# A causal depthwise convolution as a 287-point transform on TensorE, with scale and shift formed k-tile by k-tile beside the first product

## The chip, the cores and the metric

The kernel runs on one core of a Trainium2 chip. The metric is device microseconds of one execution; a lower number is better. In this text PE is TensorE (matmuls) and PEld its weight loads, DVE is VectorE, ACT is ScalarE, POOL is GpSimd, and SP is SyncE, whose queue issues every large transfer. Each engine works through its own instructions in the order in which they were written out.

## The reference

Two layers work on 256 tokens of 2048 channels in float32. Layer 0 mixes tokens with a convolution module, layer 1 with gated linear attention; behind each mixer stands a feed-forward block. The part that matters here is the beginning of layer 0:

```python
mod = silu(c) @ w_ada[i] + b_ada[i]                 # c: one row of 2048; w_ada: 2048 x 12288
sh1, sc1, gt1, sh2, sc2, gt2 = split(mod, 6)
h = rms_norm(x, pre_mix_g[i]) * (1.0 + sc1) + sh1
u = h @ w_pw1 + b_pw1                               # 2048 -> 4096, "pw1"
a, g = split(u, 2); u = a * sigmoid(g)
u = depthwise_conv(u, w_dw, 31 taps, causal) + b_dw # each channel by itself
u = silu(layer_norm(u, ln_g, ln_b))
y = u @ w_pw2 + b_pw2                               # 2048 -> 2048, "pw2"
x = x + gt1 * rms_norm(y, post_mix_g[i])
h = rms_norm(x, pre_ffn_g[i]) * (1.0 + sc2) + sh2   # then the feed-forward block
```

The products are computed with float32 split in two parts of reduced precision, hi and lo, as hi·hi + hi·lo + lo·hi. A causal convolution of 256 tokens with 31 taps has 286 outputs, so a circular transform of 287 points holds it without wrapping.

## The kernel before, in words

Channels lie on the 128 partitions in 16 k-tiles, tokens along the row. All weights come from HBM as tiles of 128 x 2048 numbers (1 MiB), in one long list that `tile_order()` writes out by hand; `pump_one()` takes the next entry, issues its transfer on SP and writes the work that goes with it. There are six buffers (`rawp`), so a transfer waits until the sixth tile before it has been used. A weight tile of a product is turned into two halves of hi (a cast on ACT, L281) and lo (a subtraction, L282); for pw1 the subtraction is on POOL, for all other products on DVE. `product()` runs the matmuls of one product in the order of `ORDERS`; for pw1 the weights are the stationary operand and 256 tokens stream through (L342, L343, L348), so its output has channels as rows.

Scale and shift (`mod`) come in two ways. An `ada` tile holds the weights of 128 outputs and is one DVE instruction (L260), a product with silu(c) and a sum along the row. An `adap` tile is k-tile k of a whole chunk of 2048 outputs and goes through PE (`ada_rows`, L214): silu(c) is the stationary operand in 32 columns, and four matmuls of 512 columns go to four column groups of the array. Of layer 0, SC1 and SH1 are `ada` tiles at the very start; GT1, SC2 and SH2 are `adap` tiles beside pw1 and pw2. As soon as all of SC1 and a block of SH1 are there, `modulate()` forms h of one k-tile: mt on DVE (L414), hi on ACT (L417), lo on DVE (L418).

The convolution follows pw1 block by block (`conv_done`): a sigmoid and a bias on ACT, their product on POOL or DVE, and then 31 taps, each one DVE instruction on 128 x 256 numbers into PSUM (L623, L604 for the last two blocks, where 4 and 12 taps are diagonal matmuls on PE, L591). Mean and mean square of the layer norm are gathered on PE (`conv_sums`, L567). Behind the last block a short chain forms the normalisation, and pw2 begins (L318 to L320 in packed blocks, L345 and L348 after them). `gather()` collects what the junction needs: sums of y, z and x·z. The junction `j0` forms the next h, and the first feed-forward product starts (the tile `in_pair`).

The scheduler of the tile framework sets the final order on each engine; blocks marked with `tc.high_priority` are drawn forward.

Of the kernel before, what the change touches and what calls it, by code (L numbers as in the profile page):

```python
# [34 lines left out]
PE_TAPS = {KD - 2: 4, KD - 1: 12}  # L35
# [3 lines left out]
PE_CHUNKS = (GT1, SC2, SH2)  # L39
PW1_GROUP = 4  # L40
# [7 lines left out]
PW1_OBS = [ob for i in range(KD) for ob in (i, KD + i)]  # L48
# [3 lines left out]
def ffn_in_obs(half):  # L52
# [4 lines left out]
    "pw1": block_order(PW1_OBS, KD, PW1_GROUP),  # L57
# [24 lines left out]
def tile_order():  # L82
# [40 lines left out]
def trunk(ctx: ExitStack, tc: tile.TileContext, a: dict, out: bass.AP):  # L123
# [15 lines left out]
    early = pre.enter_context(tc.tile_pool(name="early", bufs=1))  # L139
    ccol = early.tile([P, KD], F32, tag="ccol", name="ccol")  # L140
    nc.sync.dma_start(out=ccol, in_=a["ccol"])
    cc = early.tile([P, KD, 32], F32, tag="cc", name="cc")
    ident = const.tile([P, P], F32, tag="ident", name="ident")
    x = const.tile([P, KD, T], F32, tag="x", name="x")
    par = const.tile([P, NCOLS], F32, tag="par", name="par")
    masks = const.tile([P, 8, P], I8, tag="masks", name="masks")
# [8 lines left out]
    quad = early.tile([P, 4], F32, tag="quad", name="quad")  # L155
    nc.vector.memset(quad, 0.0)
    for j in range(4):
        nc.vector.memset(quad[32 * j : 32 * j + 32, j : j + 1], 1.0 / 32)
# [16 lines left out]
    der = const.tile([P, 8, KD], F32, tag="der", name="der")  # L175

# [21 lines left out]
    def chunk_done(layer, chunk):  # L198
        m = modcol(layer, chunk * KD, KD)
        kinds = {SC1: (0, "pre_mix_g"), GT1: (1, "post_mix_g"), SC2: (2, "pre_ffn_g"), GT2: (3, "post_ffn_g")}  # L200
        if chunk in kinds:
            kind, g = kinds[chunk]
            nc.vector.scalar_tensor_tensor(
                out=der[:, layer * 4 + kind, :], in0=m, scalar=1.0 if kind in (0, 2) else 0.0,
                in1=cols(g, layer * KD, KD), op0=ALU.add, op1=ALU.mult,
            )

    rows = {}

    def ada_rows(raw, n, k):  # L210
        if k == 0:
            rows[n] = ps2.tile([P, 512], F32, tag="ss", name=f"ada{n}")
        for j in range(4):
            nc.tensor.matmul(  # L214
                rows[n][32 * j : 32 * j + 32, :], cc[:, k, :], raw[:, j * 512 : (j + 1) * 512],
                start=k == 0, stop=k == KD - 1,
            )
        if k < KD - 1:
            return
        got = rows.pop(n)  # L220
        flat = rawp.tile([P, TILE * P], F32, tag="raw", name=f"flat{n}")[:, :512]
        nc.scalar.copy(flat, got)
        pc = ps2.tile([P, 512], F32, tag="ss", name=f"adac{n}")[:, :KD].rearrange("p (j s) -> p s j", j=4)
        for s in range(4):
            nc.tensor.matmul(pc[:, s, :], flat[:, s * P : (s + 1) * P], quad, start=True, stop=True)
        chunk = PE_CHUNKS[n]
        nc.vector.tensor_tensor(
            out=modcol(0, chunk * KD, KD).rearrange("p (j s) -> p j s", j=4), in0=pc.rearrange("p s j -> p j s"), in1=cols("b_ada", chunk * KD, KD).rearrange("p (j s) -> p j s", j=4),
            op=ALU.add
        )  # L230
        chunk_done(0, chunk)
# [5 lines left out]
    def pump_one():  # L237
        kind, name, i = order[state["next"]]
        state["next"] += 1
        if kind == "x":  # L240
            nc.sync.dma_start(out=x, in_=a["x"])
            return
        if kind == "par":
            nc.sync.dma_start(out=par, in_=a["par"])
            nc.sync.dma_start(out=ident, in_=a["ident"])
# [7 lines left out]
        if kind == "adap":  # L253
            nc.sync.dma_start(out=raw, in_=a["w_ada_d"][name, i])
            waiting.append((state["emitted"], lambda: ada_rows(raw, name, i)))
            return
        if kind == "ada":
# [5 lines left out]
            if i % KD == KD - 1 or (name, i // KD) == (0, SH1):  # L263
                first = i if i // KD == SH1 and name == 0 else i - KD + 1
# [4 lines left out]
                if i % KD == KD - 1:  # L269
                    chunk_done(name, i // KD)  # L270
            if (name, i // KD) == (0, SH1):
                modulate(i % KD, rbx, 0, 0, SH1)
            return
        nc.sync.dma_start(out=raw, in_=a[name][i])
        on_pool = name == "pw1"
        eng = nc.gpsimd if on_pool else nc.vector
        for j in range(2):
# [4 lines left out]
            done = eng.tensor_tensor(out=lo, in0=part, in1=hi.bitcast(F32), op=ALU.subtract)  # L282
            last_lo[:] = [] if on_pool else [done.ins]
# [160 lines left out]
    def gather_on(stack, ob, name, yo, **kw):  # L444
# [8 lines left out]
        else:  # L453
            square_into(s_y, yo, f"{name}_y{ob}", ob == 0, **bias)
        nc.vector.tensor_scalar(
            out=z, in0=yo, scalar1=kw.get("bias", 0.0), scalar2=aa, op0=ALU.add, op1=ALU.mult
        )
# [58 lines left out]
    ssx = None  # L516
    pump(-1)
    while order[state["next"]][0] != "w" and order[state["next"]] != ("ada", 0, SH1 * KD):
        pump_one()
    ssx = new_ss("ssx")[:, :2]  # L520
    for k in range(KD):
        sq = new_sq(f"x_sq{k}")
        nc.scalar.square(sq, x[:, k, :])
        sum_sq(ssx, sq, inv_d, k == 0, k == KD - 1)
    rbx = rstd(ssx, "nx")

    with tc.tile_pool(name="conv", bufs=1) as cv:
        dw = cv.tile([P, KD, WIDTH], F32, tag="dw", name="dw")
        nc.sync.dma_start(out=dw, in_=a["dw"])
        uc = cv.tile([P, KD, T], F32, tag="uc", name="uc")  # L530
        up = [cv.tile([P, PAD + T], F32, tag=f"up{i}", name=f"up{i}") for i in range(4)]
        for u in up:
            nc.vector.memset(u[:, :PAD], 0.0)
        w128 = cv.tile([P, P], F32, tag="w128", name="w128")
        nc.vector.memset(w128, 1.0 / P)
        base = cv.tile([P, T], F32, tag="base", name="base")
        stat = {}
        first = {}
        later = []
# [417 lines left out]
```

## Time and profile before

| | |
|---|---|
| median of three runs | 2446.92 us (2445.59 to 2451.66) |
| the profiled execution | 2445.52 us, of which its span 2443.7 us |
| PE busy | 2340.2 us, 96% of the span |
| DVE busy | 1832.0 us, 75% |
| ACT, POOL busy | 1112.5 us, 200.4 us |
| read from HBM | 599.89 MB, 246 GB/s over the span |

Busy shares are means over the span. The span begins with the first instruction. An engine that is busy may still be waited for by none; what a stage costs is read from the chain of waits, which goes back from the last instruction and says at each step what released it. A matmul's length in the profile is a modelled one that overlaps with the next; the distance from one start to the next is what it costs in a row of them.

### The profile page before, as it was taken

The numbers are of one execution on the slowest core, as the hardware profiler recorded it, in microseconds if no ns is written. First come the engines' busy times: TensorE is split into PE (matmuls) and PEld (weight loads), VectorE is DVE, ScalarE is ACT, GpSimd is POOL, SyncE is SP. The second block draws the span as 40 slices with busy tenths as digits, with TensorE's granted clock in tenths as the row PEclk, the third lists the DMA queues.
The fourth block names the chain that finished last, engine by engine and source line by source line (L and its number), as shares of the span: only waits on it lengthen the run. The fifth ranks groups of instructions, "written<-read, shape, count | busy, mean of one in ns | idle before, by whom it ended". The sixth has DMA issues, their size and how long they took to land.

```text
span 2443.7 us, 36498 instructions
## 1 busy us (share of the span) xinstructions
PE 2340.2 (96%) x14554; PEld 2051.4 (84%) x14554; DVE 1832.0 (75%) x2784; ACT 1112.5 (46%) x1679; POOL 200.4 (8%) x118
## 2 busy tenths in 40 slices
PE   3599999899999999999999999999999999999997
PEld 2588868798888888888888989988988888888886
DVE  7988876887777677878986987889666655665665
ACT  2244425554444444444445545454444444444442
POOL 0377730000000000000000000000000000000001
PEclk9899999899999999999999999999999999999999
DMA  9877788557778777877843566784556665665651
GB/s 396 333 277 261 273 334 294 199 176 289 286 286 303 288 290 294 294 293 290 297 172 138 207 256 233 285 295 140 207 207 225 223 218 211 224 218 202 220 189 68
DMA packets 84157, 604.36 MB, mean 247 GB/s; under 512 B 9473, under 2 KB 9857, under 8 KB 11025
## 3 DMA queue, kind: packets, MB, share of 16 engines
q1 hardware_dynamic: 83986, 602.02, 67.5%
q8 instruction: 114, 1.87, 0.3%
q14 instruction: 57, 0.47, 0.1%
HBM read 599.89 MB, written 2.10 MB: 246 GB/s over the span
## 4 chain that ended last, share of the span: by engine, by line
PE 93%; DVE 4%; DMA 1%; ACT 1%; POOL 1%; issue 1%; SPq 0%; POOLq 0%; DVEq 0%; ACTq 0%
PE in L345 24%; PE out L345 13%; PE in L348 12%; PE out L348 7%; PE pw L348 3%; PE pw L342 3%; PE pw L343 2%; PE wo L345 2%; PE ada L214 2%; DVE raw L260 2%; PE in_pair L318 1%; PE r L342 1%; PE in_pair L319 1%; PE r L343 1%; PE r L348 1%; PE in_pair L320 1%
## 5 line engine op out<-in xcount | busy, mean ns | idle before, releaser
L281 ACT CAST hi<-raw 128x1024 fp32r<-128x1024 f32 x754 | 790.8, 1050 | 1080.8 <-issue 292.1
L282 DVE TENSOR_TENSOR lo<-raw,hi 128x1024 fp32r<-128x1024 f32 x690 | 844.1, 1224 | 498.0 <-ACT hi L281 496.3
L345 PE MATMUL in<-h,hi 128*128 128x512 f32 x2560 | 896.3, 396 | 0.1
L348 PE MATMUL in<-h,lo 128*128 128x256 f32 x2560 | 715.8, 280 | 0.0
L345 PEld LDWEIGHTS in<-h,hi 128*128 128x128 f32 x2560 | 480.2, 188 | 114.7 <-DVE gate L690 0.3
L348 PEld LDWEIGHTS in<-h,lo 128*128 128x128 f32 x2560 | 482.7, 189 | 0.0
L345 PE MATMUL out<-m,hi 128*128 128x512 f32 x1364 | 477.3, 394 | 0.0
L348 PE MATMUL out<-m,lo 128*128 128x256 f32 x1408 | 392.0, 281 | 0.0
L260 DVE SCALAR_TENSOR_TENSOR raw<-raw,cb 128x2048 f32<-128x2048 f32 x144 | 328.7, 2286 | 13.3 <-ACT cb L152 8.1
L345 PEld LDWEIGHTS out<-m,hi 128*128 128x128 f32 x1364 | 254.9, 188 | 58.5
L348 PEld LDWEIGHTS out<-m,lo 128*128 128x128 f32 x1408 | 264.1, 188 | 2.0
L623 DVE SCALAR_TENSOR_TENSOR ca<-up,dw,ca 128x256 f32<-128x256 f32 x420 | 170.9, 484 | 24.5 <-ACT ca L621 23.0
L342 PE MATMUL pw<-h,hi 128*128 128x256 f32 x528 | 155.6, 303 | 32.9 <-ACT hi L281 28.6
L348 PE MATMUL pw<-h,lo 128*128 128x256 f32 x640 | 183.0, 292 | 3.0 <-POOL lo L282 3.0
L282 POOL TENSOR_TENSOR lo<-raw,hi 128x1024 fp32r<-128x1024 f32 x64 | 156.9, 2454 | 123.7 <-ACT hi L281 106.8
L343 PE MATMUL pw<-h,hi 128*128 128x256 f32 x528 | 154.4, 295 | 11.4 <-DVE h L418 11.4
L342 PEld LDWEIGHTS pw<-h,hi 128*128 128x128 f32 x528 | 103.8, 201 | 60.8 <-ACT hi L281 29.7
L348 PEld LDWEIGHTS pw<-h,lo 128*128 128x128 f32 x640 | 125.1, 198 | 10.6 <-issue 5.4
L343 PEld LDWEIGHTS pw<-h,hi 128*128 128x128 f32 x528 | 105.7, 201 | 14.2 <-DVE h L418 13.3
L345 PE MATMUL wo<-oo,hi 128*128 128x512 f32 x240 | 83.7, 394 | 0.0
L318 PE MATMUL in_pair<-h,hi 128*128 128x256 f32 x256 | 71.4, 291 | 2.9 <-ACT h L417 2.9
L417 ACT ACTIVATE h<-mt,mod 128x256 fp32r<-128x256 f32 x64 | 31.2, 505 | 93.2 <-DVE mod L266 74.5
(328 smaller groups left out, 3074.1 us busy)
## 6 DMA issues: line engine op xcount, KB each, us to landing
raw<-in_in_dram SPq DMA_DIRECT2D x176, 1024.0 KB, 5.0
raw<-in_w_ada_dram SPq DMA_DIRECT2D x144, 1024.0 KB, 5.7
raw<-in_out_dram SPq DMA_DIRECT2D x88, 1024.0 KB, 5.3
raw<-in_pw_dram SPq DMA_DIRECT2D x48, 1024.0 KB, 6.9
raw<-in_w_ada_d_dram SPq DMA_DIRECT2D x48, 1024.0 KB, 5.6
raw<-in_aqk_dram SPq DMA_DIRECT2D x17, 1024.0 KB, 5.0
raw<-in_v_dram SPq DMA_DIRECT2D x16, 1024.0 KB, 5.2
raw<-in_r_dram SPq DMA_DIRECT2D x16, 1024.0 KB, 5.9
```

The costliest lines, as they stand in the source:

```text
L214: nc.tensor.matmul(rows[n][32 * j : 32 * j + 32, :], cc[:, k, :], raw[:, j * 512 : (j + 1) * 512], start=k == 0, stop=k == KD - 1,)
L260: nc.vector.scalar_tensor_tensor(out=raw, in0=raw, scalar=1.0, in1=cb, op0=ALU.mult, op1=ALU.mult, accum_out=modcol(name, i))
L281: nc.scalar.copy(hi, part)
L282: done = eng.tensor_tensor(out=lo, in0=part, in1=hi.bitcast(F32), op=ALU.subtract)
L318: nc.tensor.matmul(acc, w_hi, x_hi, start=opens, stop=False, skip_group_check=True)
L319: nc.tensor.matmul(acc, w_hi, x_lo, start=False, stop=False, skip_group_check=True)
L342: nc.tensor.matmul(acc[:, :T], w_hi[:, s], x_hi, start=n == 0, stop=False)
L343: nc.tensor.matmul(acc[:, :T], w_hi[:, s], x_lo, start=False, stop=False)
L345: nc.tensor.matmul(acc, w_hi[:, s], pair.rearrange("p a b -> p (a b)"), start=n == 0, stop=end, skip_group_check=True)
L348: nc.tensor.matmul(acc[:, :T], w_lo[:, s], x_hi, start=False, stop=end, skip_group_check=ob not in narrow)
L417: nc.scalar.activation(out=h_hi[:, k, :], in_=t, func=AF.Identity, bias=sh)
L623: nc.vector.scalar_tensor_tensor(out=ca, in0=u[:, w : w + T], scalar=cw, in1=ca, op0=ALU.mult, op1=ALU.add)
```

## The change

- **Convolution.** The taps are transformed once at the start (12 matmuls, `turn`). After pw1, 512 channels at a time: u = a·sigmoid(g) on DVE, forward matmuls against `fwd` on PE (L616), the product of two spectra on DVE (seven instructions for 256 channels, L625 to L633), and the way back against `inv` (L643 to L645), all in plain float32. 128 of the 144 frequencies are held as real and imaginary parts in `fab`, the other 16 in `fr`. The 31-tap chains, their POOL and PE parts and `conv_sums` are gone.
- **pw1** has tokens as output rows: h is the stationary operand and 512 output channels stream through (L695 to L697), in eight chunks of 512. Three chunks (4, 0, 5) run k-tile by k-tile in the head, the other five (1, 6, 2, 7, 3) after it. A bias matmul opens each (L688). The subtraction for lo is on DVE.
- **Scale and shift.** SC1 and SH1 are now "rows": a unit is 2 MiB and gives 128 outputs of SH1 and of SC1 through PE, 16 matmuls of 256 columns in four column groups (L246), a copy on ACT (L253), two matmuls that fold the four partial sums into a column (L255), and then der, mt and h of that k-tile. So the list has, for each k-tile, two tiles of rows and 0.75 tile of pw1 (twelve tiles in all, "twelve blocks"). GT1 and half of SH2 are rows too, behind pw1 and beside pw2; SC2 and the other half of SH2 are `ada` tiles on DVE beside pw1 and pw2.
- **Smaller things.** The squares of x are formed in four large pieces at the start and kept as s_xx, so `gather_x` in pw2 is gone. In pw2 z moves from DVE to ACT. The layer norm's sums go as s_z and s_y on DVE. x, par and ident are loaded first.

The core of the diff:

```diff
-PE_TAPS = {KD - 2: 4, KD - 1: 12}
-PE_CHUNKS = (GT1, SC2, SH2)
+WIDE = 512
+HEAD_CHUNKS = (4, 0, 5)
+TAIL_CHUNKS = (1, 6, 2, 7, 3)
+NF = 287
+ROW_UNITS = [(k, KD + k) for k in range(KD)]
+ROW_UNITS += [(GT1 * KD + k, GT1 * KD + k + 1) for k in range(0, KD, 2)]
+ROW_UNITS += [(SH2 * KD + k, SH2 * KD + k + 1) for k in range(0, 8, 2)]
...
-    order = ada(0, SC1)
-    order[2:2] = [("par", 0, 0)]
-    order[4:4] = [("x", 0, 0)]
-    shift = ada(0, SH1)
-    order += shift[:4] + pw1[:1] + shift[4:7] + pw1[1:2] + shift[7:10] + pw1[2:3] + shift[10:13] + pw1[3:4] + shift[13:]
-    order += spread(pw1[PW1_GROUP:], late[:26]) + late[26:36]
-    order += spread(pw2[:10], late[36:]) + pw2[10:]
+    for k in range(KD):
+        order += rows(k)
+        order += [pw1[i] for i in range(lead) if 4 * i // len(HEAD_CHUNKS) == k]
+    late = ada(0, SC2) + ada(0, SH2)[8:]
+    order += spread(pw1[lead:], late[:18])
+    order += rows(*units[:6])
+    order += spread(pw2[:12], rows(*units[6:]) + late[18:], 4) + pw2[12:]
...
+        for i in range(HALF):
+            k = half * HALF + i
+            j = 32 * (k % 4)
             nc.tensor.matmul(
-                rows[n][32 * j : 32 * j + 32, :], cc[:, k, :], raw[:, j * 512 : (j + 1) * 512],
-                start=k == 0, stop=k == KD - 1,
+                bank[j : j + 32, :T], cc[:, k, :], wv[:, i, :], start=k < 4, stop=k >= KD - 4
             )
...
-        eng = nc.gpsimd if on_pool else nc.vector
-            done = eng.tensor_tensor(out=lo, in0=part, in1=hi.bitcast(F32), op=ALU.subtract)
+            done = nc.vector.tensor_tensor(out=lo, in0=part, in1=hi.bitcast(F32), op=ALU.subtract)
...
+            for part, dst in enumerate((fab[:, :T], fab[:, T:], fr)):
+                for t in range(2):
+                    nc.tensor.matmul(
+                        dst, fwd[:, t, part * F_MAIN : part * F_MAIN + n], u[:, t, :], start=t == 0, stop=t == 1
+                    )
+            nc.vector.tensor_tensor(out=va, in0=fa, in1=ha, op=ALU.mult)
...
+                    nc.tensor.matmul(yi, va[:, i, :], inv[:, 0, :], start=True, stop=False)
+                    nc.tensor.matmul(yi, vb[:, i, :], inv[:, 1, :], start=False, stop=False)
+                    nc.tensor.matmul(yi, v2[:rows, sel], inv[:rows, 2, :], start=False, stop=True)
...
+        for t in range(2):
+            n = slice(t * P, (t + 1) * P)
+            nc.tensor.matmul(accs[c][t], h_hi[:, k, n], w_hi[:, s], start=False, stop=False)
+            nc.tensor.matmul(accs[c][t], h_hi[:, k, n], w_lo[:, s], start=False, stop=False)
+            nc.tensor.matmul(accs[c][t], h_lo[:, k, n], w_hi[:, s], start=False, stop=k == KD - 1)
```

How it moves the instructions is shown at three places. First PE in the head, where h of the first k-tiles becomes ready. Before, PE has only the first four blocks of pw1 there (the tile pw, by output block):

```order
L396 MATMUL nx_rb<-nx_dg,ones 128x256
L342 MATMUL pw_0_372<-h,hi_330 128x256
L343 MATMUL pw_0_372<-h,hi_330 128x256
L342 MATMUL pw_16_376<-h,hi_330 128x256
L343 MATMUL pw_16_376<-h,hi_330 128x256
```

Now each k-tile's sums (ada, from two raw tiles) stand between the products of the k-tile before, here in the middle of the head; pw_40 and pw_41 are the two token halves of chunk 4:

```order
L255 MATMUL ada_478<-dup,flat_497 128x1 x2
L246 MATMUL ada_543<-raw_541,cc 32x256 x8
L246 MATMUL ada_543<-raw_552,cc 32x256 x8
L695 MATMUL pw_40_289<-hi_448,h 128x512
L696 MATMUL pw_40_289<-lo_449,h 128x512
L695 MATMUL pw_41_290<-hi_448,h 128x512
```

So PE does the sums and the product in turn, where it did only the product.

Second, DVE beside pw1. Before, it holds the tap chains of two blocks in turn:

```order
L623 SCALAR_TENSOR_TENSOR ca_890<-up_261,dw,ca_890 128x256
L623 SCALAR_TENSOR_TENSOR ca_1064<-up_262,dw,ca_1064 128x256
L623 SCALAR_TENSOR_TENSOR ca_890<-up_261,dw,ca_890 128x256
L623 SCALAR_TENSOR_TENSOR ca_1064<-up_262,dw,ca_1064 128x256
L623 SCALAR_TENSOR_TENSOR ca_890<-up_261,dw,ca_890 128x256
```

Now it holds the subtractions for lo, the sums of SC2 and the products of spectra (va, vx, vb) side by side:

```order
L319 TENSOR_TENSOR lo_1258<-raw_1255,hi_1257 128x1024
L300 SCALAR_TENSOR_TENSOR raw_1326,mod<-raw_1326,cb 128x2048
L625 TENSOR_TENSOR va_1154<-fab_1147,y 128x256
L626 TENSOR_TENSOR vx_1156<-fab_1147,y 128x256
L629 TENSOR_TENSOR vb_1155<-fab_1147,y 128x256
```

So each subtraction that PE waits for is now queued behind such sums and products.

Third, PE between the last matmul of pw1 and the inverse of the last chunk. Before, the last matmuls of the taps (pt) and of the statistics stand there with a few sums:

```order
L348 MATMUL pw_31_3133<-h,lo_2930 128x256
L225 MATMUL adac_3077<-quad,flat_3075 128x4 x4
L214 MATMUL ada_3086<-raw_3063,cc 32x512 x4
L214 MATMUL ada_3086<-raw_3069,cc 32x512 x4
L591 MATMUL pt_3202<-up_262,diag_283 128x256 x9
```

Now the sums of three whole units (2156, 2182, 2208) stand between the forward part of the last chunk (the rows of fab and fr) and its way back:

```order
L616 MATMUL fr_2291<-u_2327,fwd 64x256 x2
L255 MATMUL ada_2130<-dup,flat_2149 128x1 x2
L246 MATMUL ada_2156<-raw_2128,cc 32x256 x8
L246 MATMUL ada_2156<-raw_2139,cc 32x256 x8
L255 MATMUL ada_2156<-dup,flat_2175 128x1 x2
L246 MATMUL ada_2182<-raw_2154,cc 32x256 x8
L246 MATMUL ada_2182<-raw_2165,cc 32x256 x8
L255 MATMUL ada_2182<-dup,flat_2201 128x1 x2
L246 MATMUL ada_2208<-raw_2180,cc 32x256 x8
L246 MATMUL ada_2208<-raw_2191,cc 32x256 x8
L255 MATMUL ada_2208<-dup,flat_2227 128x1 x2
L643 MATMUL back_2310<-inv,va_2299 128x256
```

So the way back is now queued behind six tiles that must have landed.

More of the change, by code (lines that the diff above doesn't have):

```diff
@@ L56 @@
 ORDERS = {
-    "pw1": block_order(PW1_OBS, KD, PW1_GROUP),
+    "pw1": [(4 * c + j, k) for c, k in PW1_CHUNKS for j in range(4)],
     "pw2": block_order(list(range(KD)), KD, HEAD),
@@ L206, in chunk_done, with have @@
             )
+        if (layer, chunk) == (0, GT1):
+            nc.vector.tensor_tensor(out=ab, in0=der[:, 1, :], in1=cols("conv_b_pw2", 0, KD), op=ALU.mult)
     rows = {}
[L210 to L213, printed above, removed]
+    missing = {(l, c): KD for l in range(2) for c in range(6)}
+    def have(layer, chunk, n):
+        missing[layer, chunk] -= n
+        if not missing[layer, chunk]:
+            chunk_done(layer, chunk)
@@ L217, in ada_rows @@
             )
-        if k < KD - 1:
+        if half == 0:
             return
[L220 to L226, printed above, removed]
+        rows.pop(u)
@@ L229, in ada_rows @@
-            op=ALU.add
-        )
-        chunk_done(0, chunk)
+            out=mod[:, sel], in0=bank[:, T : T + 2], in1=par[:, b_at + n0 : b_at + n1 + 1 : n1 - n0], op=ALU.add
+        )
+        if u < KD:
+            nc.vector.scalar_tensor_tensor(
+                out=der[:, 0, u : u + 1], in0=modcol(0, n1), scalar=1.0, in1=col("pre_mix_g", u),
+                op0=ALU.add, op1=ALU.mult,
+            )
+            modulate(u, rbx, 0, 0, SH1)
+            return
+        have(0, n0 // KD, 2)
@@ new lines, in trunk @@
+    v2s = [cv.tile([P, T], F32, tag=f"v2{j}", name=f"v2{j}") for j in range(2)]
+    for v2 in v2s:
+        nc.vector.memset(v2[4 * F_REST : 4 * F_REST + 32, :], -1.0 / 32)
+    for c in range(4):
+        chans = taps[:, c * WIDE : (c + 1) * WIDE]
+        for part in range(3):
+            n = min(F_MAIN, F_COLS - part * F_MAIN)
+            pt = ps.tile([P, WIDE], F32, tag="mm", name=f"taps{c}{part}")[:n, :]
+            nc.tensor.matmul(pt, turn[:, part * F_MAIN : part * F_MAIN + n], chans, start=True, stop=True)
+            if part == 2:
+                nc.scalar.copy(h2[:, c * WIDE : (c + 1) * WIDE], pt)
+            else:
+                nc.scalar.copy(
+                    y[:, 4 * c : 4 * c + 4, part * P : (part + 1) * P], pt.rearrange("p (b n) -> p b n", n=P)
+                )
@@ new lines, in trunk @@
+    sqs = [rawp.tile([P, TILE * P], F32, tag="raw", name=f"sqs{j}") for j in range(2)]
+    quarter = [sqs[j // 2][:, (j % 2) * 4 * T : (j % 2 + 1) * 4 * T] for j in range(4)]
+    for j in range(4):
+        nc.scalar.square(quarter[j], x[:, 4 * j : 4 * j + 4, :].rearrange("p a b -> p (a b)"))
+        if j % 2:
+            nc.vector.tensor_tensor(out=quarter[j - 1], in0=quarter[j - 1], in1=quarter[j], op=ALU.add)
+    nc.vector.tensor_tensor(out=quarter[0], in0=quarter[0], in1=quarter[2], op=ALU.add)
@@ new lines, in trunk @@
+        if k == KD - 1:
+            pw1_done(c, accs.pop(c))
+    run_waiting(state["used"])
+    while order[state["next"]][0] == "rows":
+        pump_one()
+        if len(waiting) > 2:
+            waiting.pop(0)[1]()
+    run_waiting(state["used"])
+    with tc.high_priority(offset=CRITICAL):
+        pm = ps2.tile([P, 512], F32, tag="acc", name="l_pm", bufs=2)[:, :4]
+        sum_sq(pm[:, :2], s_z, inv_d, True, False)
+        sum_sq(pm[:, 2:], s_y, inv_d, False, False)
+        sum_sq(pm[:, :2], y[:, KD - 1, :], inv_d, False, True)
+        sum_sq(pm[:, 2:], ends["u"], inv_d, False, True)
```

361 lines of the change are left out of this document (193 added, 168 removed).

## The prediction

> **What bounds the kernel now.** I read the run by stages first, since the shares of the whole span mix stages with different limits. The windows are cut at the points the chain of waits gives: end of the scale sums, first product (pw1), normalisation, second product (pw2), junction, and all that follows. The columns are window, length, busy time of PE, its weight loads, DVE, ACT and POOL, the granted clock, the DMA share and GB/s.
>
> ```profile
> 0.00:37.00 37.00, 21.16 (x72) 16.30 (x72) 21.89 (x41) 17.71 (x41) 2.90 (x5) 1.00 0.94 381
> 37.00:118.60 81.60, 34.06 (x162) 29.05 (x162) 79.58 (x93) 14.67 (x22) 22.53 (x8) 0.89 0.88 355
> 118.60:357.40 238.80, 237.85 (x1762) 189.04 (x1766) 197.43 (x480) 93.44 (x140) 153.74 (x84) 0.99 0.77 288
> 357.40:368.40 11.00, 7.87 (x45) 2.83 (x41) 8.82 (x20) 3.96 (x7) 0.69 (x1) 0.76 0.85 329
> 368.40:472.40 104.00, 104.00 (x744) 90.01 (x744) 81.99 (x159) 60.25 (x108) 0.00 (x0) 0.99 0.76 272
> 472.40:488.30 15.90, 8.52 (x34) 7.02 (x33) 10.01 (x30) 4.85 (x11) 1.54 (x2) 0.61 0.19 66
> 488.30:2443.70 1955.40, 1926.71 (x11742) 1717.13 (x11742) 1432.26 (x1969) 917.59 (x1352) 18.99 (x18) 0.99 0.65 235
> ```
>
> For 118 us PE waits: DVE is busy 79.58 of 81.60 us in the second window. Then PE is the bound for 239 and 104 us. Everything after 488.3 us is untouched, so the case is decided by when the first feed-forward matmul starts. The chain of waits (start, length, what) names the same limits; its rows at the seams:
>
> ```profile
> 99.80 2.21 DVE raw L260 x2
> 113.10 0.48 DVE h L418
> 118.65 0.58 PE pw L343
> ...
> 358.64 2.35 DVE lo L282 x2
> 364.24 2.06 PE nl_rb L396 x4
> 368.35 1.22 PE pw_pair L318 x4
> ...
> 476.41 1.87 PE j_my L370 x8
> 478.28 4.27 PE j_m L370 x20
> 488.25 1.22 PE in_pair L318 x4
> ```
>
> The first 118 us are thus 32 scale and shift sums of one DVE instruction each (L260), with loads at full speed behind them.
>
> **Prices.** The groups of instructions by line, and a window in which transfers were the limit:
>
> ```profile
> L623 DVE SCALAR_TENSOR_TENSOR ca<-up,dw,ca 128x256 f32<-128x256 f32 x420 | 170.9, 484 | 24.5 <-ACT ca L621 23.0
> L282 POOL TENSOR_TENSOR lo<-raw,hi 128x1024 fp32r<-128x1024 f32 x64 | 156.9, 2454 | 123.7 <-ACT hi L281 106.8 <-PE ada L214 15.2 <-PE pbase L555 1.0
> L260 DVE SCALAR_TENSOR_TENSOR raw<-raw,cb 128x2048 f32<-128x2048 f32 x32 | 72.8, 2288 | 13.3 <-ACT cb L152 8.1 <-DMA raw<-in_w_ada_dram 5.2
> L282 DVE TENSOR_TENSOR lo<-raw,hi 128x1024 fp32r<-128x1024 f32 x44 | 53.7, 1223 | 23.1 <-ACT hi L281 22.9
> L434 DVE TENSOR_TENSOR s_z<-s_z,p_z 128x256 f32<-128x256 f32 x14 | 5.9, 420 | 0.1
> 20.00:60.00 40.00, 13.15 (x57) 12.25 (x57) 35.99 (x39) 9.60 (x29) 2.70 (x1) 1.00 1.01 419
> ```
>
> At 419 GB/s one tile of 1 MiB costs 2.50 us. PE's prices come from start-to-start distances in the timeline (start, length, instruction):
>
> ```profile
> 469.42 0.28 PE L342 MATMUL pw<-h,hi 128*128 128x256 f32 x1
> 472.18 0.28 PE L348 MATMUL pw<-h,lo 128*128 128x256 f32 x1
> ...
> 1379.77 0.39 PE L825 MATMUL v<-lo,h 128*128 128x512 f32 x1
> 1383.43 0.39 PE L826 MATMUL v<-hi,h 128*128 128x512 f32 x1
> ...
> 422.19 0.28 PE L320 MATMUL pw_pair<-h,lo 128*128 128x256 f32 x1
> 422.40 3.64 PE L214 MATMUL ada<-raw,cc 128*32 128x512 f32 x32
> 425.98 0.50 PE L345 MATMUL pw<-h,hi 128*128 128x512 f32 x1
> 426.32 0.28 PE L348 MATMUL pw<-h,lo 128*128 128x256 f32 x1
> ...
> 325.76 1.68 PE L591 MATMUL pt<-up,diag 128*128 128x256 f32 x7
> 431.90 0.79 PE adac L225 x8
> 2.56 7.16 PE L151 MATMUL cb<-crow,ones 1*128 1x512 f32 x8 [2.56 <-DMA crow<-in_c_dram]
> ```
>
> The first pair is 23 steps in 2.76 us: 0.12 per 256-column matmul. The second, from the v product, which already has tokens as output rows, is 16 steps in 3.66 us: 0.229 per 512 columns. The row sums (L214) take 3.58 us for 16 matmuls (two passes each) of 512 columns, 0.224 each, because four column groups run side by side. An excursion from the product into them and back costs another 0.34 us (0.21 instead of 0.12 going in, 0.34 instead of 0.229 coming out, 0.14 inside). A full-width matmul in plain float32 of 256 columns is two passes of 0.215 (1.68 less the last one's length of 0.39, over the six before), so 0.43. A tiny one is 0.1 per pass (0.79 for 8).
>
> **The change, part by part.**
>
> *Removed.* 420 tap instructions on DVE (171 us), the 64 POOL subtractions (157 us), the first 32 DVE sums. None sat on the path between 118 and 357 us, where PE was busy 237.85 of 238.80, so by itself this removal buys nothing; it is the head that is freed.
>
> *Start.* 12 tap transforms of 512 columns stand on PE ahead of everything. PE is cold there: the cb row has 8 passes in 7.16 us, 0.85 each, against 0.45 for the four-wide pass above. 24 passes × 0.85 = 20.5 us after cb's 9.7, so 30.2; bias rows, sums and the reciprocal add 4, the first unit runs cold for 2 more: the head begins at about 36 us. x and par move to the front of SP's queue, ahead of nothing that is due sooner. The trace shows no matmul of 31 rows; warm, 24 passes would be half as long and the head would begin at 26.
>
> *Head (k-tile loop).* PE, from the order: 288 product matmuls × 0.229 = 66; 256 row sums of 256 columns, half of 0.224 each, 28.7 (if time went by count and not by columns, 57); 32 fold matmuls in two passes, 6.4; 21 excursions × 0.34 = 7.1. Sum 108 us, 6.8 per k-tile. Transfers: 2.75 MiB per k-tile, 6.9 us; 39 tiles are left when the first buffers come free at 36, so the last lands at 36 + 97 = 133 to 136 and its work takes 8 more. Both limits say 144. DVE has 1.5 subtractions (1.8 us) and the modulation per k-tile, ACT 1.5 casts: neither is near 6.8. Behind each fold stand mod, der, mt, h on DVE and ACT, about 1.8 us by the rows of 0.48, and up to one subtraction of 1.22 ahead of them on DVE; PE has six product matmuls and the next unit's sums in between, 1.4 + 2.1 = 3.5 us. Cost of that wait: nothing, while the next unit's tiles have landed.
>
> *Tail.* 480 products × 0.229 = 110; ten bias matmuls 2.3; 36 forward and 40 inverse matmuls × 0.43 = 32.7; one unit 2.2; 21 excursions 7.1: 154 us, so the last product matmul starts at 298. DVE has there 40 subtractions × 1.22, 18 sums × 2.29 and some 78 small operations × 0.42: 49 + 41 + 33 = 123 of 154 us, 80%, against 83% before. The subtraction is now queued behind sums that wait for a transfer, and PE waits for the subtraction.
>
> *Before pw2.* On PE: 96 row sums 10.8, 24 transform matmuls 10.3, folds 2, eight statistics matmuls 16 passes at the junction's 0.23, 3.7, the spread 2.1: 29 us, and DVE's two halves of products lie inside. Before it was 11 us. The inverse of the last chunk is queued behind three units whose six tiles must have landed: that is what is late next. pw2 starts at 327 instead of 368.
>
> *pw2 and junction.* PE's pw2 work is alike: 12 tiles of sums (48 × 0.224 = 10.8) become 80 × 0.112 = 9 plus five folds, 104 us again, so 431. DVE loses two of about seven operations per block; its backlog after the last matmul (s_z, join, y, s_y ahead of the 476.41 row) shrinks by some 3 us, junction 13: the feed-forward starts at 444.
>
> *Waits of an in-order PE.* No row shows this mix. From 118 to 357 us PE lost 1 us in 239 with DVE at 83%; in the window before it, PE worked 34 of 82 us. Nearest is the former, but its subtractions ran on POOL with nothing ahead of them; I take 12 us, with 0 and 40 as ends. Feed-forward start 456 against 488, a gain of 32.
>
> The profiled execution took 2445.52 us (span 2443.7 plus 1.8), 1.4 under the median 2446.92. 2445.5 − 32 = 2413.5; I say 2414.
>
> **A page against a row.** The cb row shows PE cold through 7.16 us without a gap. The Trainium skill (TensorE: Matmul & The Clock Gate, part 1) says the clock is doubled after about 3.4 us of sustained matmuls. By that rule the tap transforms would end near 21 us; by the row, near 30. The row's matmuls have one active row, the taps' 31, so the rule may still hold for them.
>
> **Rivals.**
> 1. PE warms during the taps. The head begins at 26 and is then bound by transfers: 26 + 41 × 2.5 + 10 = 138 instead of 144, so 2408. Against it: the cb row. This is the way of the clock gate page named above.
> 2. Row sums cost by count. Four column groups at 0.224 each whatever the width: 448 × 0.112 = 50 us more, a start at 506 and 2464, slower. It decides from 0.18 per matmul (0.112 + 32/448) on. Against it: passes of 256 columns in the pt row take 0.215, half of a 512-column one, and the weight loads of these sums leave no gap in the 3.58 us.
> 3. The modulation's chain is not covered: each k-tile pays its 1.8 + 1.2 us, 16 × 3.0 = 48 in place of 12 us of waits: 2450, no change. For it: six 1 MiB buffers for 2.75 per k-tile, and an in-order PE; in the second window PE, fed the same way, was idle most of the time. Against it: there DVE was full, here it is not.
> 4. DVE and the tiles for the units before pw2 hold PE up in the tail: twelve tiles are 30 us of transfer within some 40 us. 20 us more: 2434.
>
> **How the numbers follow.** Forecast 0.55 (2401 to 2430 with waits of 0 to 28 us), rival 1 0.15, rival 4 0.13, rival 3 0.11, rival 2 0.06. The range 2398 to 2440 leaves out rivals 2 and 3 and little else. Three runs before lie within 0.25%, so I call 0.3%, 7.3 us, what can be told from no change: faster (under 2439.6) 0.84, same 0.09, slower 0.07.
>
> **What would show it.** In the profile after: 512-column pw matmuls 0.229 apart; row sums of 256 columns near 0.112; PE above 90% busy and transfers near 400 GB/s from about 40 to 140 us; the last pw1 matmul near 300 to 310, in_pair near 456, and an unchanged 1955 us after it. It is wrong if PE idles several us in each k-tile, or if the row sums cost 0.2.

## The result and the profile after

The changed kernel takes 2458.32 us (median of 11 runs, 2451.51 to 2465.76), against 2446.92 us before (11 runs). The ratio is 1.0047 with a 95% interval of 1.0035 to 1.0060: slower, by about 11 us, where 33 us less was forecast. The profiled execution took 2462.36 us, its span 2460.6 us, 4 us above its median.

First the windows of the changed kernel, cut at its own seams: the cb matmuls; most of the tap transforms; their end and the first two units of row sums; the head from the first product matmul to the last; the tail to the last pw1 matmul; the gap before pw2; pw2; the junction; all that follows. The columns are those of the prediction's windows.

```profile
0.00:10.00 10.00, 7.16 (x8) 2.47 (x8) 0.79 (x9) 6.70 (x9) 0.20 (x4) 1.00 0.71 241
10.00:40.00 30.00, 18.06 (x19) 4.65 (x20) 10.18 (x8) 12.09 (x16) 0.00 (x0) 1.00 0.56 195
40.00:59.00 19.00, 19.00 (x123) 8.14 (x121) 4.64 (x9) 5.27 (x11) 0.70 (x1) 1.00 0.88 330
59.00:173.40 114.40, 103.74 (x760) 74.39 (x761) 46.72 (x85) 35.97 (x53) 0.00 (x0) 0.97 0.96 376
173.40:328.30 154.90, 154.90 (x679) 118.07 (x678) 111.77 (x154) 56.05 (x73) 0.00 (x0) 1.00 0.74 268
328.30:372.20 43.90, 32.34 (x283) 19.23 (x282) 19.07 (x50) 11.46 (x21) 0.69 (x1) 0.97 0.76 287
372.20:489.10 116.90, 110.92 (x843) 97.26 (x840) 82.36 (x137) 66.54 (x117) 0.00 (x0) 0.95 0.76 289
489.10:499.20 10.10, 6.31 (x36) 4.66 (x34) 6.59 (x20) 3.21 (x6) 1.54 (x2) 0.68 0.31 104
499.20:2460.50 1961.30, 1932.27 (x11742) 1719.55 (x11742) 1431.64 (x1969) 917.84 (x1352) 18.84 (x18) 0.99 0.65 234
```

The feed-forward now starts at 499.2 us, 11 us later than before (488.25); 456 was forecast. Set against the forecast, the difference falls on these stages:

| Stage | forecast, us | after, us | difference |
|---|---|---|---|
| start, to the first row sum | 36 | 48.2 | +12.2 |
| head, to its last product matmul | 108 | 125.2 | +17.2 |
| tail | 154 | 154.9 | +0.9 |
| gap before pw2 | 29 | 43.9 | +14.9 |
| pw2 | 104 | 116.9 | +12.9 |
| junction | 13 | 10.1 | -2.9 |
| allowance for waits | 12 | in the rows above | -12.0 |
| the rest | 1955.4 | 1961.3 | +5.9 |
| sum | 2411.4 | 2460.5 | +49.1 |

The forecast's 36 holds 2 us for a first unit run cold; in the trace these lie behind the first row sum, and so in the head. What lies behind the four large rows is read from the chain and the waits. The start, from the chain (start, length, what):

```profile
2.22 22.91 DMA x<-in_x_dram
...
25.16 3.90 ACT sqs L582 x4
...
29.57 11.56 PE taps L571 x12
...
43.23 3.89 PE taps L571 x4
...
48.27 2.71 PE ada L246 x22
```

The 2 MiB of x take 22.9 us to land. Behind them on ACT stand the squares of x, and behind those the copies that empty the banks of the tap transforms, so PE waits for x by way of ACT's queue. While this goes on, the transfers run at a share of 0.56 and 195 GB/s (second window), where the kernel before had 0.94 and 381 in its first 37 us.

What PE waited for, by releaser (engine, line, what; total us, times, longest): first in the head, then in the gap, then in pw2.

```profile
PE pw L695 <- ACT h L454: 9.7, 8, 1.7
...
PE ada L246 <- DMA raw<-in_w_ada_r_dram: 4.0, 2, 3.6
PE back L643 <- ACT y L656: 3.4, 3, 1.7
PE ada L255 <- ACT flat L253: 2.1, 4, 0.5
PE ada L246 <- DVE mod L261: 1.0, 3, 0.4
...
PE pw L382 <- ACT hi L318: 3.7, 2, 1.9
PE pw L385 <- DVE lo L319: 2.2, 3, 1.4
```

In the head the product waits for h at 8 of the 16 k-tiles. The timeline of PE there (start, length, instruction, idle before it) shows how little stands between the fold (L255) and the next product:

```profile
122.06 1.52 PE L697 MATMUL pw<-hi,h 128*128 128x512 f32 x6
123.43 0.50 PE L255 MATMUL ada<-dup,flat 128*128 128x1 f32 x4
123.86 2.15 PE L246 MATMUL ada<-raw,cc 128*32 128x256 f32 x32
127.45 0.50 PE L695 MATMUL pw<-hi,h 128*128 128x512 f32 x1 [1.45 <-ACT h L454]
```

After the fold comes one unit's sums (its 32 passes run from 123.86 for 2.15 us) and no product: the chain mod, der, mt, h is 1.45 us longer than its cover. The forecast had counted six product matmuls into the cover, but at these k-tiles they stand ahead of the fold. The chain is longer than forecast too: 3.6 us from 123.86 to the product, against 1.8 and at most one subtraction of 1.22. On DVE two subtractions stand in it here, one ahead of mod (1.23 us from 123.84) and one between mod and der (1.21 us from 125.06).

The gap, from the chain:

```profile
338.28 1.98 PE ada L246 x32
...
340.71 0.62 PE ada L255 x4
...
341.63 1.98 PE ada L246 x32
...
343.63 9.27 DMA raw<-in_pw_dram
...
352.92 1.04 ACT hi L318
353.96 0.38 ACT y L656
...
354.39 0.70 PE back L643 x2
```

The units go one after another, 3.35 us from start to start for 1.98 us of sums: the next unit begins only when the bank of the last has been copied, folded and read by mod. Then ACT stands at a cast (hi) that waits for a pw2 tile, with the copy y behind it for which the way back waits. By the waits above, 3.1 of the 11.6 us that PE is idle in the gap belong to the bank's chain (flat and mod), 3.4 to the copy y and 4.0 to two row tiles that come late; the rest are small ones.

### The profile page after: what moved, and what is told of

It is laid out like the page before. It is cut to its first block, busy times and chain, and to the rows that moved or that the text cites. A ratio compares the mean times of both kernels' runs of the same rounds, so it can differ in the third digit from the quotient of the medians.

```text
span 2460.6 us, 35900 instructions
## 1 busy us (share of the span) xinstructions
PE 2384.7 (97%) x14480; PEld 2048.4 (83%) x14480; DVE 1713.8 (70%) x2436; ACT 1115.1 (45%) x1655; POOL 22.0 (1%) x26
## 4 chain that ended last, share of the span: by engine, by line
PE 93%; DVE 3%; DMA 2%; ACT 1%; issue 1%; POOL 0%; POOLq 0%; SPq 0%; DVEq 0%; ACTq 0%
PE in L382 24%; PE out L382 13%; PE in L385 12%; PE out L385 7%; PE pw L695 3%; PE pw L696 2%; PE wo L382 2%; PE pw L697 2%; PE ada L246 2%; PE in_pair L355 1%; PE in_pair L356 1%; PE in_pair L357 1%; PE r L379 1%; PE r L380 1%; PE r L385 1%; PE wo L385 1%
## 5 line engine op out<-in xcount | busy, mean ns | idle before, releaser
L319 DVE TENSOR_TENSOR lo<-raw,hi 128x1024 fp32r<-128x1024 f32 x754 | 921.0, 1223 | 564.4 <-ACT hi L318 562.4
L300 DVE SCALAR_TENSOR_TENSOR raw<-raw,cb 128x2048 f32<-128x2048 f32 x136 | 310.6, 2284 | 4.8 <-DMA raw<-in_w_ada_dram 4.8
L695 PE MATMUL pw<-hi,h 128*128 128x512 f32 x256 | 101.9, 411 | 9.7 <-ACT h L454 9.7
L696 PE MATMUL pw<-lo,h 128*128 128x512 f32 x256 | 103.7, 406 | 0.0
L697 PE MATMUL pw<-hi,h 128*128 128x512 f32 x256 | 90.4, 396 | 0.0
L355 PE MATMUL in_pair<-h,hi 128*128 128x256 f32 x256 | 71.4, 293 | 2.9 <-ACT h L454 2.9
L385 PE MATMUL r<-h,lo 128*128 128x256 f32 x256 | 73.2, 286 | 0.0
L379 PE MATMUL r<-h,hi 128*128 128x256 f32 x256 | 73.1, 286 | 0.0
L380 PE MATMUL r<-h,hi 128*128 128x256 f32 x256 | 72.9, 285 | 0.0
L356 PE MATMUL in_pair<-h,hi 128*128 128x256 f32 x256 | 72.6, 290 | 0.0
L695 PEld LDWEIGHTS pw<-hi,h 128*128 128x128 f32 x256 | 49.3, 193 | 27.2 <-ACT h L454 13.9
L385 PE MATMUL wo<-oo,lo 128*128 128x256 f32 x256 | 71.2, 281 | 0.0
```

The costliest lines, as they stand in the source:

```text
L300: nc.vector.scalar_tensor_tensor(out=raw, in0=raw, scalar=1.0, in1=cb, op0=ALU.mult, op1=ALU.mult, accum_out=modcol(name, i))
L319: done = nc.vector.tensor_tensor(out=lo, in0=part, in1=hi.bitcast(F32), op=ALU.subtract)
L355: nc.tensor.matmul(acc, w_hi, x_hi, start=opens, stop=False, skip_group_check=True)
L356: nc.tensor.matmul(acc, w_hi, x_lo, start=False, stop=False, skip_group_check=True)
L379: nc.tensor.matmul(acc[:, :T], w_hi[:, s], x_hi, start=n == 0, stop=False)
L380: nc.tensor.matmul(acc[:, :T], w_hi[:, s], x_lo, start=False, stop=False)
```

## The experiments

All results in one table; the gain over the changed kernel is the difference of the two ratios to before, times 2447 us, since not all ran on the same chip. Executions of one kernel spread over up to 14 us, and each has one trace, which can lie off the median (experiment 1: 2437.68 against 2445.58 us); times are read from the medians, stages from the trace.

| Kernel | median, us | ratio to before | 95% interval | gain over after, us |
|---|---|---|---|---|
| after | 2458.32 | 1.0047 | 1.0035 to 1.0060 | |
| 1 taps padded to 32 rows | 2445.58 | 0.9987 | 0.9975 to 0.9998 | 15 |
| 2 taps padded to 128 rows | 2438.67 | 0.9959 | 0.9945 to 0.9974 | 22 |
| 3 sums one k-tile ahead | 2454.0 | 1.0019 | 1.0009 to 1.0028 | 7 |
| 4 six units into the tail | 2453.0 | 1.0010 | 0.9997 to 1.0024 | 9 |
| 5 six SH2 sums into the tail | 2456.23 | 1.0034 | 1.0022 to 1.0045 | 3 |
| 6 two PSUM banks in turn | 2447.1 | 0.9996 | 0.9984 to 1.0009 | 12 |
| 7 = 2 + 3 | 2433.38 | 0.9943 | 0.9926 to 0.9959 | 25 |
| 8 = 2 + 3 + 4 + 5 | 2422.23 | 0.9892 | 0.9875 to 0.9909 | 38 |
| 9 = 2 + 3 + 6 | 2421.53 | 0.9884 | 0.9868 to 0.9901 | 40 |
| 10 = 2 + 3 + 4 + 5 + 6 | 2416.36 | 0.9869 | 0.9855 to 0.9884 | 44 |

**1. One row more.** The tap table and the transform's matrix get a 32nd row of zeros.

```diff
-    taps = rawp.tile([P, TILE * P], F32, tag="raw", name="taps")[:WIDTH, :]
+    taps = rawp.tile([P, TILE * P], F32, tag="raw", name="taps")[:32, :]
...
-    turn = early.tile([P, F_COLS], F32, tag="turn", name="turn")[:WIDTH, :]
+    turn = early.tile([P, F_COLS], F32, tag="turn", name="turn")[:32, :]
...
```

> Only the taps and their transform matrix get a 32nd row of zeros. Theory (one slow transfer): the 31-row loads run on one of the 16 DMA engines, and the share of x, par and the bias rows that lies behind them on that engine waits; with 32 rows the taps land before 8 us, x near 10 instead of 25 us, the first row sums start at 36 to 40 us instead of 48.2, and the whole is 8 to 15 us shorter than the changed kernel. Rival (cold TensorE): the 24 passes at 0.85 us set the start, not the transfer; the row sums start within 4 us of 48 and the time stays within 3 us.

It took 2445.58 us, 15 us less for one row of zeros. Its second window, from 10 to 24 us:

```profile
10.00:24.00 14.00, 14.00 (x16) 3.55 (x14) 9.37 (x7) 9.80 (x13) 0.00 (x0) 1.00 0.94 368
```

PE works through, transfers are back at 0.94 and 368 GB/s, and the squares of x begin at 11.0 us instead of 25.2. The taps run from 9.6 us on instead of 20.4, the first row sum starts at 35.4 instead of 48.2. So the 31-row tables alone cost the first 13 us. It is also the start that the forecast had put at 36.

**2. The same with 128 rows.** 97 rows of zeros.

```diff
...
-    turn = early.tile([P, F_COLS], F32, tag="turn", name="turn")[:WIDTH, :]
+    turn = early.tile([P, F_COLS], F32, tag="turn", name="turn")[:128, :]
...
```

> As with 32 rows, but the taps and their matrix have 128 rows, 97 of them zero (0.9 MiB more to load). Theory (rows wake the clock): the clock stays low because only 31 of 128 rows are active; with 128 rows the passes fall from 0.85 to 0.43 us within 5 us of the first, the transforms end some 8 us earlier, less about 2 us of loading, so the time is 4 to 8 us below that with 32 rows. Rival (zeros and plain float32 do not count, or rows do not matter): all 24 passes stay at 0.85 us and the time is 0 to 3 us above that with 32 rows.

The price of the tap matmuls in the three kernels, from the groups of the first 47 us (shapes, count, busy us, mean ns, idle before); first the changed kernel, then 32 rows, then 128:

```profile
L571 PE MATMUL taps<-taps,turn 31*128 31x512 f32 x16 | 15.8, 1114 | 12.2 <-DMA turn<-in_turn_dram 10.6 <-ACT y L575 1.6
```

```profile
L571 PE MATMUL taps<-taps,turn 32*128 32x512 f32 x16 | 15.3, 1096 | 0.0
```

```profile
L571 PE MATMUL taps<-taps,turn 128*128 128x512 f32 x16 | 9.5, 726 | 0.0
```

The first two never leave the slow pace, the third does soon. The trace's clock records begin, at full speed, at 52.4, 37.8 and 13.0 us, and at the same times the matmuls get shorter. That is 4.2, 2.4 and 3.2 us after the start of the first run of wide matmuls with 128 active rows, which is a row sum in the first two (48.2 and 35.4) and a tap matmul in the third (9.7). (Four matmuls of 128 rows and a single column, 1.0 us in all, had come 6 us earlier in the first two, at 42.2 and 29.4.) With 32 rows PE had by then been busy without a gap for more than 25 us. With more zero rows another 7 us are gained. Where between 32 and 128 rows the change lies was not tried.

**3. Sums one k-tile ahead.** The list names the rows of k-tile k+1 ahead of the product of k.

```diff
+    order += rows(0)
     for k in range(KD):
-        order += rows(k)
+        order += rows(k + 1) if k + 1 < KD else []
```

> The rows of k-tile k+1 stand ahead of the pw1 tile of k-tile k in the list, so their sums and h are formed one step earlier. Theory (exposed chain): TensorE waits some 1.5 us per k-tile for h behind its fold (mod, der, mt, h); one step ahead the head from the first product to the last of chunk 5 shrinks from 117 to 105 to 110 us and the whole by 5 to 10 us. Rival (transfers set the head): at 402 to 419 GB/s from 60 to 148 us nothing is gained, the time stays within 3 us.

Its head, from the first product on, and what PE still waits there for h:

```profile
58.60:166.20 107.60, 104.39 (x760) 70.01 (x761) 48.16 (x86) 37.14 (x55) 0.00 (x0) 1.00 0.99 401
```

```profile
PE pw L696 <- ACT h L455: 0.6, 1, 0.6
```

The wait for h falls from 9.7 to 0.6 us and the stretch from 114.4 to 107.6 us. So the wait was one of order, not of durations. The transfers' share is now 0.99: the head has reached its other limit. It ends 7.2 us earlier (166.2 against 173.4), but the feed-forward starts only 5.2 us earlier (494.0 against 499.2): in this trace the clock is at half speed for 23.9 us from 344.8 on, in the gap, and in the changed kernel for 6.8 us from 369.8 on.

**4. The six units of the gap go into the tail.**

```diff
-    order += spread(pw1[lead:], late[:18])
-    order += rows(*units[:6])
+    mixed = spread([[t] for t in late[:18]], [rows(u) for u in units[:6]])
+    mixed = [t for part in spread([[t] for t in pw1[lead:]], mixed) for t in part]
+    order += mixed
```

> The six units of rows that stood between pw1 and pw2 are spread through the tail of pw1. Theory (late tiles and a serial fold chain in the gap): the stretch from the last pw1 matmul to the first of pw2 shrinks from 43.7 to 25 to 30 us, the tail grows by 6 x 2.3 = 14 us less what was there already (2 units, 4 us), the transfers beside pw2 come earlier and pw2 shrinks by 5 to 10 us: 10 to 20 us less in all. Rival (given back): DVE and the transfers are full in the tail once 50 tiles go through it, it grows by 25 us or more and the time stays within 4 us.

Tail and gap of this kernel:

```profile
174.80:342.70 167.90, 165.56 (x824) 123.17 (x822) 109.19 (x156) 56.80 (x77) 0.00 (x0) 1.00 0.74 280
342.70:367.50 24.80, 19.97 (x122) 12.55 (x120) 14.92 (x40) 9.29 (x16) 0.69 (x1) 1.00 0.59 224
```

The gap falls by 19 us, but the tail grows by 13, since PE is full there and the units' own matmuls move with them. Only the waits are gained: 11.6 us of idle PE in the gap became 4.8 in the gap and 2.3 in the tail. The medians say 9 us, and the ten executions spread from 2444 to 2456, so part of that has no place in this one trace. The expectation had the gap right and the tail 3 us too short; what failed is pw2, which was to shrink by 5 to 10 us and takes 117.5 us against 116.9.

**5. Six of the sums on DVE go from pw2 into the tail.**

```diff
-    order += spread(pw1[lead:], late[:18])
+    order += spread(pw1[lead:], late)
-    order += spread(pw2[:12], rows(*units[6:]) + late[18:], 4) + pw2[12:]
+    order += spread(pw2[:12], rows(*units[6:]), 4) + pw2[12:]
```

> Only the six remaining shift sums (SH2, one DVE instruction of 2.29 us each) move from beside pw2 to the tail of pw1. Theory (DVE crowded in pw2): between 440 and 460 us DVE is busy 20.00 of 20 and TensorE waits for hi and lo behind the sums; without them pw2 with the junction shrinks from 127 to 115 to 120 us, the tail (DVE 80%) grows by less than 3 us, 5 to 10 us less in all. Rival (transfers): pw2 is late because its tiles are queued behind row tiles in the same list; it shrinks by less than 3 us.

A miss: some 3 us (the intervals of after and of this kernel overlap). Its gap and its pw2:

```profile
331.20:377.50 46.30, 38.65 (x266) 23.17 (x264) 15.87 (x44) 10.67 (x20) 0.69 (x1) 0.78 0.65 250
377.50:491.20 113.70, 110.95 (x856) 96.90 (x857) 73.06 (x131) 66.72 (x119) 0.00 (x0) 0.97 0.68 250
```

pw2 is 3.2 us shorter, as far as the waits go that the sums had caused (hi and lo: 5.9 us before this edit, 1.7 after). But the gap is 2.4 us longer, and its granted clock is 0.78 instead of 0.97: the clock is at half speed for 17.1 us from 353.2 on, amid PE's waits, where the changed kernel has 6.8 us from 369.8 on. Experiments 3 and 7 have such a stretch too (23.9 and 13.7 us). PE's idle time in the gap is not longer here (7.7 us against 11.6), so why the clock falls earlier is not shown. The edit also takes six transfers out of pw2 with the six sums, so by itself it does not part the two theories; the chain of the changed kernel from 425 us on goes through DVE and names no transfer.

**6. Two PSUM banks in turn** for the units before pw2, and another bank for the way back of the last chunk.

```diff
-            rows[u] = ps2.tile([P, 512], F32, tag="rb" if u < KD and u % 2 else "ss", name=f"ada{u}")
+            rows[u] = ps2.tile([P, 512], F32, tag="rb" if u % 2 else "ss", name=f"ada{u}")
-                back = ps2.tile([P, 512], F32, tag="ss", name=f"back{half}")
+                back = ps2.tile([P, 512], F32, tag="acc" if half >= 6 else "ss", name=f"back{half}", **({"bufs": 2} if half >= 6 else {}))
```

> Only PSUM banks change: units of rows alternate between two banks after the head too, and the way back of the last chunk has two banks. Theory (serial chain in the gap): each unit there takes 3.4 us for 2.3 us of work since the next one waits for its bank to be folded and read, and the way back waits 3.4 us for its single bank; the stretch from the last pw1 matmul to the first of pw2 shrinks from 43.9 by 4 to 7 us. Rival (transfers): the row tiles and the first pw2 tiles arrive no sooner, so TensorE waits for them instead and the stretch shrinks by less than 2 us.

It gains 12 us, more than was expected. Tail and gap:

```profile
169.90:331.60 161.70, 161.70 (x783) 121.72 (x782) 112.11 (x156) 57.13 (x76) 0.00 (x0) 1.00 0.76 278
331.60:359.80 28.20, 25.12 (x179) 15.59 (x178) 16.20 (x44) 10.29 (x18) 0.69 (x1) 0.94 0.75 304
```

The gap is 28.2 us, and the forecast had said 29. That the two agree is luck: the 29 have six units in them, this gap has three (96 of 192 passes). PE no longer waits for a tile there, and for ACT and DVE only 3.1 us instead of 7.5. The tail is 6.8 us longer, as the sums of this tile show (a line for the group in the tail: duration, first and last start):

```profile
L246 PE MATMUL ada<-raw,cc x128: 379/379/404, 308.6 to 328.2; 128*32 128x256 f32 x128
```

128 passes, four units, now run inside the tail, where the changed kernel has one unit: with the second bank the scheduler has drawn three more forward. This edit moves work too, then, and its 12 us can't be put down to the bank's chain alone.

**7. 128 rows and sums ahead together.**

> 128-row taps, and rows one k-tile ahead. Theory (the chain behind the fold sets the late head): both gains add, the 288th product matmul starts near 147 us instead of 154.4 with padding alone and 166.2 with the lead alone; 5 to 7 us below padding alone. Rival (transfers set the head at 2.6 us per tile): with the start already early, the lead brings under 2 us more.

2433.38 us: 25 us of the 22 + 7, and 4 us below the padding alone, between the 5 to 7 of the theory and the 2 of the rival. The intervals of experiments 2 and 7 overlap, so the times don't settle how much the lead adds here. The head from its first product:

```profile
32.50:144.70 112.20, 107.51 (x791) 69.86 (x792) 50.00 (x87) 37.33 (x56) 0.00 (x0) 1.00 1.00 409
```

Head and start end at 144.7 us; the forecast had said 144, with a start that was 10 us later. Here the transfers are the bound: share 1.00, and 112.2 us at 409 GB/s are 45.9 MB, or 44 tiles of 1 MiB. The head uses 44 as well, but these are not the same ones, since transfers run ahead of their use by up to six buffers.

**8. The padding (2) and the three edits of the order (3, 4 and 5),** with all 24 sums of DVE in the tail.

> 128-row taps, rows one k-tile ahead, all shift and scale sums and the first six units of rows in the tail of pw1. Theory: the four costs are separate, so the gains add: 20 (start) + 5 (lead) + 5 (gap) + 5 to 8 (pw2) below the changed kernel, 2420 to 2426 us, and about 1% under the kernel before. Rival (one limit behind them all, DVE at over 85% and transfers at over 350 GB/s in the tail): the tail grows by 15 us or more and the time stays above 2430.

2422.23 us, 38 us below the changed kernel and 26 below the kernel before (0.9892). The sum of its parts was 22 + 7 + 9 + 3 = 41.

**9. 128 rows, sums ahead, two banks;** the units stay before pw2.

> 128-row taps, sums one k-tile ahead, and alternating PSUM banks for the units before pw2 and for the way back; the six units stay between pw1 and pw2. Theory (the gap is a chain through one PSUM bank, independent of start and head): the 11 us of the alternating banks add to the 2433 of the other two, so 2420 to 2426, with 26 to 30 us from the last pw1 matmul to pw2. Rival (the gap waits for the tiles of the units, and the earlier start only brings the wait forward): the gap stays at 38 us or more and the time at 2430 to 2435.

2421.53 us with a gap of 28.8 us: as the first theory said. The gap had been 46.3 us in experiment 7, so it was a matter of the order around one bank, and not of tiles that come late. Not all of these 17.5 us are waits: 128 passes run in the tail here too, which is 6.8 us longer (162.2 against 155.4), PE's idle time in the gap falls by 4.4 us (7.5 to 3.1), and the granted clock there rises from 0.82 to 0.88.

**10. Experiment 8 with two banks.**

> The combined version (six units and all 24 DVE sums in the tail of pw1) with alternating banks added. Theory: with the units gone from between pw1 and pw2 only the way back is left to gain from a second bank; its waits are about 3 us, so 2417 to 2423. Rival (the units' bank chain also costs PE in the tail, 168 us there against 155): the tail shortens by 5 us or more and the time falls to 2410 to 2416.

2416.36 us, the lowest time of all, 0.9869 of before. From the first row sum on:

```profile
26.30:150.00 123.70, 118.27 (x878) 76.39 (x879) 55.58 (x96) 42.84 (x64) 0.71 (x1) 0.99 1.01 407
150.00:312.80 162.80, 162.80 (x811) 121.28 (x810) 120.60 (x168) 53.43 (x74) 0.00 (x0) 1.00 0.84 325
312.80:337.80 25.00, 21.02 (x123) 13.99 (x121) 15.24 (x40) 9.13 (x16) 0.69 (x1) 0.84 0.71 276
337.80:447.00 109.20, 109.20 (x856) 95.83 (x857) 73.63 (x131) 66.49 (x119) 0.00 (x0) 0.97 0.70 251
```

Neither theory is borne out. The gap is 25.0 us against 25.1 in experiment 8, so the way back gained nothing; the tail (from the head's last product) is 166.6 us against 166.9, so the units gained nothing there. The profiled spans differ by 5.1 us, of which 1.3 are in pw2 and 2.6 behind the junction; the two intervals overlap, and whether the second bank is worth anything here stays open.

## Why the prediction was wrong

The sign was wrong, by four steps of the sum: start, head, gap and pw2.

**Start: "x and par move to the front of SP's queue, ahead of nothing that is due sooner", and the head begins at 36.** This step failed by 12 us. The transfers of the start were not priced at all. Two tables of 31 rows stand ahead of x, and PE waits 10.6 us for them (the first tap row in experiment 2), and then for x by way of ACT. One more row put the start at 35.4 (experiment 1). The tap price itself was a little low: from 9.6 to 34.3 us there, less 2.1 us for bias rows and sums in between, is 22.6 instead of 20.5. That 35.4 still meets the 36 is because the 2 us for a cold first unit lie behind this mark.

**The page against the row.** The row was right for this kernel: the taps stayed slow to their end. The Trainium skill (TensorE: Matmul & The Clock Gate, part 1) gives about 3.4 us of sustained matmuls; that agrees with the 128-row taps (full speed 3.2 us after the first) and not with those of 31 and 32 rows, which stayed slow through more than 20 us. Rival 1's start at 26 came about with 128 rows (first row sum at 26.2), not in the changed kernel.

**Head: the "cost of that wait: nothing" behind each fold.** Failed, with 9.7 us. At half of the k-tiles the order has all product matmuls ahead of the fold, so the cover is one unit's sums at most. Rival 3 was this mechanism, at a fifth of the price it was given (48 us). With the wait taken away (experiment 3) the head is 7.4 us shorter and still takes 117.8 us from the first row sum on, 9.8 above the forecast. Some 2 us of these are the cold first unit; the transfers, at 401 GB/s and a share of 0.99 where the forecast had put 39 tiles at 419 GB/s, are the limit that is left, and how much of the 9.8 is theirs was not tried. The PE prices held: from 80 to 140 us PE is 93% busy, as forecast, with transfers at 408 GB/s:

```profile
80.00:140.00 60.00, 55.59 (x454) 39.47 (x446) 25.21 (x46) 19.66 (x29) 0.00 (x0) 1.00 1.01 408
```

**Tail: 154 us.** Right, 154.9, and without a wait. DVE took 112 us of it, 123 were forecast. Rival 4's place was wrong: nothing held PE up in the tail; the late tiles cost 4.0 us in the gap.

**Before pw2: 29 us.** Failed, by 15. The sum of PE's work was 3 us low (32.3 us); that it would run without waits was the larger error. Of 11.6 us of waits, 3.1 come from units in turn through one bank, 3.4 from ACT's queue, where a cast that waits for a pw2 tile stands ahead of the copy that the way back needs, and 4.0 from row tiles. The prediction looked at the six tiles as what is late next; those are a third of it. With two banks PE waits 3.1 us in all.

**pw2: 104 us again.** Failed, by 13. PE waited 5.9 us for hi and lo, a wait that its paragraph on pw2 gave no place: it said only that DVE loses two of about seven operations per block, and not that SH2 sums of 2.2 us each come in among the subtractions. The chain through DVE ends so (raw is a sum and the read of its accumulator):

```profile
460.63 2.21 DVE raw L300 x2
...
464.19 1.14 DVE lo L319
465.37 0.58 PE pw L385
```

and in the stretch around it DVE has no idle time while PE works 4.4 of 7 us, at half the clock:

```profile
462.00:469.00 7.00, 4.42 (x13) 3.43 (x14) 7.00 (x15) 2.46 (x4) 0.00 (x0) 0.52 1.00 415
```

Experiments 5 and 8 bring pw2 to 113.7 and 110.5 us, with 1.7 us of that wait left. In experiment 8 no stretch of pw2 is at a low clock, and PE still works 107.9 us:

```profile
339.00:449.50 110.50, 107.85 (x856) 94.40 (x857) 73.28 (x131) 66.59 (x119) 0.00 (x0) 1.00 0.70 258
```

So PE's own work in pw2 is some 4 us more than the 104 of before, and not alike. By difference (an estimate), 3 of the 13 us are left for the stretches at half speed in the changed kernel, 4.4 us at the start of pw2 and 6.8 us from 462.0 on; this was not tried further.

**The allowance of 12 us.** PE's waits for the engines and tiles named above are 9.7 + 11.6 + 5.9 = 27 us, inside the ends of 0 and 40, nearer to the upper. The value was taken from a stage (118 to 357 us) in which no product waited for a chain through three engines; the head before, where PE did wait, was set aside because DVE had been full there.

**The rest: "unchanged 1955".** 1961.3 in the profiled execution, 1951.5 (experiment 1) to 1959.9 (experiment 9) in those of the experiments. The code is the same. The stretch at half speed at the second junction is 17.1 us long in the changed kernel and 10.2 before, but that does not explain it: experiment 3 has 17.1 us there and a rest of 1955.0, experiment 9 has 10.2 and 1959.9. The cause stays open.

**Rival 2** (row sums cost by count) was wrong: 32 passes of 256 columns take 1.86 us in the chain, 0.116 us for a matmul of two passes, where 0.112 was forecast. It named the right side for the wrong reason. No rival was a late start, but that alone did not make the range miss: with the start mended (experiment 1) the time is 2445.58 us, still above 2440. The 27 us of waits would have fitted into the range; beside them stand the 12 us of the start and what was sized too low in the head (7.5), the gap (3.3) and pw2 (7.0).

## What to carry to other kernels

Price the small transfers at a program's start as well as the large ones, by their row counts, and ask which engine's queue carries the wait on. A cover must be read in the order: what stands between the fold and the product that needs its result, at each pass of the loop, and not what stands between two folds. And where units share one PSUM bank and an in-order engine, their latencies add up even if no engine is full; here a second bank, or an order that begins the units earlier, took out much of that (PE's waits in the gap fell from 11.6 us to 3.1 and 4.8). A term that comes out at the forecast size proves little until one has counted what is in it.

## What the runs showed of the hardware

Transfers of 31 rows delayed what was issued after them: 248 KB and 39 KB took until 20.4 us, and the 2 MiB of x 22.9 us, while the share of the DMA engines was 0.56. With 32 rows x was there at 11.0 us. The Trainium skill (DMA: Bandwidth & Descriptors, on why a DMA increments its semaphore by 16) says that a transfer is split over the largest number of engines up to 16 that divides the row count, which for the prime 31 is one; these two runs agree with it.

The clock of PE was not released by matmuls of 1, 31 or 32 active rows, however long they ran without a gap (up to 25 us), and was released 2.4 to 4.2 us after the first run of wide matmuls with 128 rows began. 96 more rows of zeros made the same tap matmuls faster: 726 ns instead of 1096 on average for the 16 passes of the rows in experiment 2. The clock column of the windows does not show this: it reads 1.00 from 0 to 40 us in the changed kernel, while the durations say half speed, since the trace has no clock record before 52.4 us.
